# Reciprocal softmax sums spread over head rows by a DRAM round trip in place of 0/1 matmuls

## The chip, the cores and the metric

The kernel runs on one core of a Trainium2 chip. The metric is the device time of one execution in microseconds (us), the median of three runs; smaller is better. Engines are named as in the profile: PE (TensorE, matrix products; PEld its weight loads), DVE (VectorE), ACT (ScalarE), POOL (GpSimd), SP (SyncE, which here only issues DMAs).

## The reference

A two-layer encoder trunk for 1024 tokens of width 1024 in float32. Layer 0 mixes tokens by grouped-query softmax attention (16 query heads, 4 key/value heads of width 64), layer 1 by a chunked gMLP; each is followed by a squared-ReLU MLP, and each sub-layer is normalised, modulated and gated by a conditioning vector. What matters here:

```python
s = jnp.einsum('bqkgd,bskd->bkgqs', q_blk, k).astype(jnp.float32) * scale
p = jax.nn.softmax(s, axis=-1).astype(v.dtype)
o = jnp.einsum('bkgqs,bskd->bqkgd', p, v)
...
return o @ w_o          # added to x, times a gate
```

The softmax is written as exponentials, their product with v, and a division of every row of o by the row's sum of exponentials. The change is in how that division reaches the transposed o.

## The kernel before, in words

x is held transposed, features on partitions and tokens along the row, in two halves of 512 tokens. A float32 product is made of three fast products: each operand is split into a high part (ACT cast to fp32r) and a low part (the rest, by DVE or POOL), and hi·hi, hi·lo and lo·hi are added up in PSUM.

**Attention.** 64 units, each one head and 256 queries; the first 32 units are half 0. A unit has scores (L948) and their maximum (L951, DVE), exponentials (L957, ACT, which also leaves the row sums in `rowsum`), transposes (L965), their split (L968 ACT, L974 DVE), the product with v (L984) and copies of the output (L994, L996 ACT, L1001 POOL) into `ot`: per pair of heads `dt` and half one buffer of 128 rows (64 per head) x 512 queries, not yet divided. The stages of three neighbouring units are interleaved by the string `ORDER` (line 1784); most of them are pinned to their place on their engine. Its last item, `m00`, is where other work is slipped in, one piece a unit. The output projection's preparation for half 0 stands there from unit `WO_AT` = 53 on: at unit 53 `copy_sel`, at unit 54 `wo_sums(0)`, at units 55 to 62 `wo_prep(0, dt)` for dt = 0 to 7. Units 64 and 65 of the loop are the tail of the last two.

**The division before.** `wo_sums` takes the reciprocal of the row sums (queries on partitions, heads along the row), splits it into high and low part (L882, L883), transposes it by four PE transposes into 32 rows (16 heads, high and low) x 512 queries (L886) and copies that out of PSUM (L888, ACT). `sel` is a constant 32 x 1024 matrix of 0 and 1, loaded from DRAM (two DMAs) and cast by ACT (L875). `wo_prep(hf, dt)` multiplies 128 columns of it with the transposed reciprocals on PE (L892, the tile `bc`): every row of the 128 gets its head's reciprocals. DVE multiplies `ot` by `bc` (L894), and the result is split (L896 ACT; L897, POOL in half 0, DVE in half 1).

**The projection.** `wo_mm(m, halves)`: 24 products per half of 128x512 (L906 to L908: eight k, three products each), then DVE adds the gated result to x (L910, the evacuation), and the square of the new x is summed (L260 ACT, L264 DVE). m = 0 to 5 run for half 0 alone, m = 6 and 7 for both halves, then m = 0 to 5 for half 1. m = 0 is emitted at the attention's end. `wo_sums(1)` comes next, and `wo_prep(1, dt)` three, three and two at a time ahead of m = 1, 2, 3 (`PREP`). `mods` slips in loads and products (L145, L153, L158, L166) that make the modulation vectors of later layers.

**Weights.** `load_w` keeps one weight ahead (`AHEAD` = 1): `issue_w` has SP load a 128x1024 float32 buffer `w` (L113), ACT cast its high part (L116) and POOL take the low part (L117) into two `s` buffers. There are four `w` buffers, which the modulation's loads share, and five `s`, of which one holds the conditioning vector. SP issues in program order, and a DMA waits at the head of its queue until its buffer is free; a buffer `w` of a weight comes free with its L117, one of the modulation with its L153. A DMA also waits for the eighth DMA before it on its queue.

Of the kernel before, what the change touches and what calls it, by code (L numbers as in the profile page):

```python
# [28 lines left out]

INS = (  # L30
    "xT", "cond", "cols", "ada", "adan", "wqkv", "qkg", "wo", "wu", "wv", "bv", "ws", "bs", "wgo", "wi",
    "wm", "rope", "sel",
)


# [1 line left out]
def encoder_kernel(ctx: ExitStack, tc: tile.TileContext, t: dict, out: bass.AP):  # L37
# [3 lines left out]
    const = ctx.enter_context(tc.tile_pool(name="const", bufs=1))  # L41
    small = ctx.enter_context(tc.tile_pool(name="small", bufs=3))
    mem = ctx.enter_context(tc.tile_pool(name="mem", bufs=1))

    uid = [0]

# [4 lines left out]
    def pin(ins):  # L51
        tc.keep_in_program_order(ins)
# [7 lines left out]
    def slot(dt=F32, shape=(P, 512)):  # L60
        return mem.tile(list(shape), dt, tag="t", name=nm("t"), bufs=SLOTS["t"])
# [24 lines left out]
    def f32(ap):  # L86
        return ap.bitcast(F32)
# [771 lines left out]


    on = {}
    sel = []
    ot = {}
    rT = {}

    def load_sel():
        for i in range(2):
            raw = slot(F32, (32, 512))
            nc.sync.dma_start(raw, t["sel"][:, i * 512 : (i + 1) * 512])
            sel.append(raw)  # L870

    def copy_sel():
        for i in range(2):
            s_ = slot(F32R, (32, 512))
            pin(S.copy(s_, sel[i]))  # L875
            sel[i] = s_

    def wo_sums(hf):
        ri = small.tile([P, 4, NH], F32, tag="ri", name=nm("ri"), bufs=1)
        V.reciprocal(ri, rowsum[:, 4 * hf : 4 * hf + 4])  # L880
        rs = small.tile([P, 4, 2, NH], F32R, tag="rs", name=nm("rs"), bufs=1)
        V.tensor_copy(rs[:, :, 0], ri)  # L882
        V.tensor_tensor(rs[:, :, 1], ri, f32(rs[:, :, 0]), ALU.subtract)  # L883
        pt = bank_x("rt", (32, 512), F32R)
        for j in range(4):
            T.transpose(pt[:, j * P : (j + 1) * P], rs[:, j].rearrange("p s h -> p (s h)"), identr)  # L886
        rT[hf] = slot(F32R, (32, 512))
        S.copy(rT[hf], f32(pt))  # L888

    def wo_prep(hf, dt):  # L890
        pb = bank_x("bc")
        T.matmul(pb, sel[dt // 4][:, (dt % 4) * P : (dt % 4 + 1) * P], rT[hf], start=True, stop=True)  # L892
        o_ = ot.pop((dt, hf))
        V.tensor_tensor(o_, o_, pb, ALU.mult)  # L894
        hi, lo = slot(F32R), slot(F32R)
        S.copy(hi, o_)  # L896
        (G, V)[hf].tensor_tensor(lo, o_, f32(hi), ALU.subtract)  # L897
        on[(dt, hf)] = (hi, lo)
# [17 lines left out]
    with ExitStack() as es:  # L916
# [132 lines left out]
        for i in range(nu + 2):  # L1049
# [7 lines left out]
            for op in ORDER.split():  # L1057
                f, w, j = op[0], int(op[1]), int(op[2])
                if f == "m":
                    if i in deferred:  # L1060
                        deferred.pop(i)()
                    elif i == WO_AT - 6:
                        load_sel()
                    elif WO_AT <= i < WO_AT + 10:
                        if i == WO_AT:
                            copy_sel()
                        elif i == WO_AT + 1:
                            wo_sums(0)
                        else:
                            wo_prep(0, i - WO_AT - 2)  # L1070
                    elif i >= nu:
                        mods(1)
                    if late_mods and i % 4 == 1:
                        late_mods.pop()()
                    if i % 4 == 3 and 12 <= i < 52:
                        late_mods.append(mod_ahead())
                    slabs.step(bank_x, i >= 14 and (i % 4 in (1, 2) or i % 8 == 3))
                elif f == "q":
                    if i % 4 == 0 and w == 0 and i + 4 < nu:
                        qh = q_stage(units[i + 4].qq, units[i + 4].g)  # L1080
                    if i % 4 > 1 and w == 1 and i + 2 < nu:
                        q_trans(qh, i % 4 - 2, nxt)
                else:
                    u = (u0, u1, u2)[w]
                    if u and (i or f not in "se"):
                        stages[f](u, j)
# [6 lines left out]

    es_a.close()
    p_y = ctx.enter_context(tc.tile_pool(name="p_y", bufs=4, space=PSUM))
    dram = ctx.enter_context(tc.tile_pool(name="dram", bufs=1, space=bass.MemoryType.DRAM))

    class Out:


# [305 lines left out]
        out_.run(at_out, done)  # L1406

    wo_sums(1)
    for m in range(1, WA):
        if m == 1:  # L1410
            x[1] = [load_x(1, k) for k in range(KT)]
        for dt in PREP[m - 1] if m < 4 else ():
            wo_prep(1, dt)
        wo_mm(m, (0,), bank_y)
        mods(WOM[m])
# [371 lines left out]
def _pack(inp):  # L1787
# [35 lines left out]
    cos, sin = np.cos(ang), np.sin(ang)  # L1823
    rope = np.stack([np.concatenate([cos, cos], -1), np.concatenate([-sin, sin], -1)]).astype(np.float32)
    t["rope"] = rope.reshape(2, 8, P, HD).transpose(0, 2, 1, 3).reshape(2, P, 512)
    sel = np.zeros((32, KT, P), np.float32)
    for dt in range(KT):
        for m in range(P):
            sel[2 * dt + m // 64, dt, m] = 1.0
            sel[16 + 2 * dt + m // 64, dt, m] = 1.0  # L1830
    t["sel"] = sel.reshape(32, KT * P)
    return {k: np.ascontiguousarray(t[k]) for k in INS}


# [16 lines left out]
```

## Time and profile before

| | |
|---|---|
| time of three runs | 2626.04, 2627.94 (median), 2629.11 us |
| span of the profiled execution, first to last instruction | 2625.8 us |
| busy: PE, PEld, DVE, ACT, POOL | 2601.6, 2172.2, 2183.1, 1451.1, 723.2 us |
| mean granted TensorE clock | 0.999 of full speed |
| attention's units with work of the projection's preparation | about 470 to 555 us |
| projection, half 0 and m = 6, 7 | about 548 to 608 us |

The profiled execution's own time isn't stated beside its page; its span lies 0.2 to 3.3 us below the three times, which is what an execution has around its first and last instruction, and the scatter. How to read the rows: in a timeline, start, length, engine, line, operation, out<-in with the buffer numbers left out, and in brackets how long the engine was idle before and what released it. In the rows of groups, the total busy time and the mean ns of one, then the engine's idle time just before them. In the rows of windows, the window, its length, and for each engine its busy time and number of instructions, then the granted clock, the share of the DMA engines in use and GB/s. Lines are those of the kernel before.

### The profile page before, as it was taken

Reading aid. Unit: us, or ns where it says so; the run is one execution under the profiler, and the core shown is the slowest. Engines: PE = TensorE matmul, PEld = TensorE weight load, DVE = VectorE, ACT = ScalarE, POOL = GpSimd, SP = SyncE. Lnnn points to the kernel's source line nnn. Section 1 sums busy time; section 2 is a strip of 40 time slices with the busy share of each in tenths; the row PEclk is TensorE's granted clock in tenths of the full one; section 3 lists DMA queues with packets and bytes.
Section 4 is the critical chain, followed back from the end, with each engine's and each line's share of the span. In section 5 each row is a group of like instructions: output and inputs, shape, how many; then the busy total and the mean of one; then the engine's idle time right before and its main releaser. Section 6 shows DMA issues by size and latency. Waiting matters only on the chain. (4 is left out here: it accounts for less than half of the span.)

```text
span 2625.8 us, 37307 instructions
## 1 busy us (share of the span) xinstructions
PE 2601.6 (99%) x12860; PEld 2172.2 (83%) x12860; DVE 2183.1 (83%) x3276; ACT 1451.1 (55%) x2612; POOL 723.2 (28%) x531
## 2 busy tenths in 40 slices
PE   9999999999999999999999999999999999999999
PEld 7789999888788888888888888888888788888887
DVE  7868999887989989877897687788979977789974
ACT  4569999854654455446543354445456645465442
POOL 0238776533000004430122054451520000005400
PEclk9999999999999999999999999999999999999999
DMA  8010222234486788545243355568641554487461
GB/s 306 27 33 9 74 88 75 97 112 145 168 288 245 270 310 306 192 133 172 82 136 121 120 174 175 178 204 305 237 141 50 177 179 156 153 310 268 149 211 58
DMA packets 208752, 435.39 MB, mean 166 GB/s; under 512 B 23025, under 2 KB 35441, under 8 KB 208562
## 3 DMA queue, kind: packets, MB, share of 16 engines
q1 hardware_dynamic: 181682, 395.24, 44.7%
q10 hardware_dynamic: 26880, 37.76, 4.0%
q8 instruction: 102, 1.67, 0.3%
q14 instruction: 88, 0.72, 0.1%
HBM read 310.23 MB, written 122.68 MB: 165 GB/s over the span
## 5 line engine op out<-in xcount | busy, mean ns | idle before, releaser
L1212 PE MATMUL out<-t,s 128*128 128x512 f32 x1232 | 479.9, 390 | 0.9 <-ACT t L328 0.8
L1213 PE MATMUL out<-t,s 128*128 128x512 f32 x1232 | 479.3, 389 | 0.7 <-DVE t L329 0.7
L1214 PE MATMUL out<-t,s 128*128 128x512 f32 x1232 | 478.9, 389 | 0.0
L469 PE MATMUL w<-t,s 128*128 128x512 f32 x1168 | 459.8, 395 | 0.9 <-ACT t L328 0.5
L470 PE MATMUL w<-t,s 128*128 128x512 f32 x1168 | 455.2, 390 | 1.8 <-DVE t L329 1.8
L471 PE MATMUL w<-t,s 128*128 128x512 f32 x1168 | 454.7, 389 | 0.0
L329 DVE TENSOR_TENSOR t<-t,t 128x512 fp32r<-128x512 f32 x408 | 324.7, 806 | 36.2 <-ACT t L328 29.0
L328 ACT CAST t<-t 128x512 fp32r<-128x512 f32 x408 | 245.3, 617 | 122.2 <-DMA t<-hf 71.7
L1213 PEld LDWEIGHTS out<-t,s 128*128 128x128 f32 x1232 | 231.2, 188 | 50.2 <-DVE t L329 1.8
L1212 PEld LDWEIGHTS out<-t,s 128*128 128x128 f32 x1232 | 231.2, 188 | 50.2 <-ACT t L328 1.7
L1214 PEld LDWEIGHTS out<-t,s 128*128 128x128 f32 x1232 | 231.2, 188 | 48.1
L454 ACT CAST s<-w 128x512 fp32r<-128x512 f32 x292 | 173.4, 616 | 161.4 <-PE w L471 104.3
L470 PEld LDWEIGHTS w<-t,s 128*128 128x128 f32 x1168 | 219.3, 188 | 49.7 <-DVE t L329 5.2
L469 PEld LDWEIGHTS w<-t,s 128*128 128x128 f32 x1168 | 219.3, 188 | 49.4 <-issue 2.9
L471 PEld LDWEIGHTS w<-t,s 128*128 128x128 f32 x1168 | 219.2, 188 | 45.6
L455 DVE TENSOR_TENSOR s<-w,s 128x512 fp32r<-128x512 f32 x292 | 221.8, 766 | 41.1 <-ACT s L454 40.6
L1194 ACT CAST s<-t 128x512 fp32r<-128x512 f32 x240 | 148.2, 620 | 187.0 <-PE out L1214 136.3
L1180 POOL TENSOR_TENSOR w<-w,t 128x512 f32<-128x512 f32 x20 | 34.2, 1721 | 767.7 <-DMA t<-hf 691.5
L1195 DVE TENSOR_TENSOR s<-t,s 128x512 fp32r<-128x512 f32 x240 | 195.1, 814 | 56.1 <-ACT s L1194 55.4
L951 DVE TENSOR_REDUCE mx<-s 128x1 f32<-128x1024 f32 x128 | 156.2, 1220 | 30.5 <-PE s L948 29.2
L974 DVE TENSOR_TENSOR t<-t,t 128x512 fp32r<-128x512 f32 x256 | 164.1, 681 | 17.1 <-ACT t L968 16.4
L984 PE MATMUL o<-t,t 128*128 128x256 f32 x1024 | 162.6, 291 | 0.0
(251 smaller groups left out, 5089.1 us busy)
## 6 DMA issues: line engine op xcount, KB each, us to landing
t<-hf SPq DMA_DIRECT2D x320, 256.0 KB, 4.0
hf<-c SPq DMA_DIRECT2D x156, 256.0 KB, 3.4
w<-in_wi_dram SPq DMA_DIRECT2D x64, 512.0 KB, 4.5
hf<-c ACTq DMA_DIRECT2D x96, 256.0 KB, 2.7
w<-in_ada_dram SPq DMA_DIRECT2D x36, 512.0 KB, 3.9
x<-in_ada_dram SPq DMA_DIRECT2D x64, 256.0 KB, 5.4
t<-in_wm_dram SPq DMA_DIRECT2D x64, 256.0 KB, 4.7
wf<-w SPq DMA_DIRECT2D x64, 256.0 KB, 3.0
```

Source lines behind the costliest of these rows:

```text
L328: S.copy(hi, src)
L329: (eng or V).tensor_tensor(lo, src, f32(hi), ALU.subtract)
L454: S.copy(hi, src)
L455: V.tensor_tensor(lo, src, f32(hi), ALU.subtract)
L469: T.matmul(ps, hi[:, a], th, start=kt == 0, stop=False)
L470: T.matmul(ps, hi[:, a], tl, start=False, stop=False)
L471: T.matmul(ps, lo[:, a], th, start=False, stop=kt == 3)
L974: pin(V.tensor_tensor(lo, pt, f32(hi), ALU.subtract))
L1195: V.tensor_tensor(lo, src, f32(hi), ALU.subtract)
L1212: T.matmul(ps, hi[:, a], th, start=begin and kt == 0, stop=False, **g)
L1213: T.matmul(ps, hi[:, a], tl, start=False, stop=False, **g)
L1214: T.matmul(ps, lo[:, a], th, start=False, stop=end and kt == 3, **g)
```

## The change

The reciprocals are transposed as plain float32, 16 rows x 512 queries, copied out by ACT, and stored to a DRAM tile `rd`. For each pair of heads two DMAs read one row of it each, 64 times over, into the two halves of a 128x512 buffer; DVE multiplies `ot` by that buffer, in SBUF. `sel`, its loads and casts, the split of the reciprocals and the sixteen `bc` products are gone. In half 0 `wo_sums(0)` is at unit 53, the loads for dt = 0 to 7 at units 54 to 61, each one unit ahead of its `wo_prep`, which stay at units 55 to 62. In half 1 all eight pairs of loads are issued behind `wo_sums(1)`, ahead of the loop over m.

```diff
     def wo_sums(hf):
         ri = small.tile([P, 4, NH], F32, tag="ri", name=nm("ri"), bufs=1)
         V.reciprocal(ri, rowsum[:, 4 * hf : 4 * hf + 4])
-        rs = small.tile([P, 4, 2, NH], F32R, tag="rs", name=nm("rs"), bufs=1)
-        V.tensor_copy(rs[:, :, 0], ri)
-        V.tensor_tensor(rs[:, :, 1], ri, f32(rs[:, :, 0]), ALU.subtract)
-        pt = bank_x("rt", (32, 512), F32R)
+        pt = bank_x("rt", (NH, 512))
         for j in range(4):
-            T.transpose(pt[:, j * P : (j + 1) * P], rs[:, j].rearrange("p s h -> p (s h)"), identr)
-        rT[hf] = slot(F32R, (32, 512))
-        S.copy(rT[hf], f32(pt))
+            T.transpose(pt[:, j * P : (j + 1) * P], ri[:, j], ident)
+        rT = slot(F32, (NH, 512))
+        S.copy(rT, pt)
+        rd[hf] = dram.tile([NH, 512], F32, name=nm("rd"))
+        nc.sync.dma_start(rd[hf], rT)
+
+    def wo_load(hf, dt):
+        rb_[(dt, hf)] = slot()
+        for i in range(2):
+            nc.sync.dma_start(rb_[(dt, hf)][64 * i : 64 * i + 64],
+                              rd[hf][2 * dt + i : 2 * dt + i + 1].broadcast_to([64, 512]))
 
     def wo_prep(hf, dt):
-        pb = bank_x("bc")
-        T.matmul(pb, sel[dt // 4][:, (dt % 4) * P : (dt % 4 + 1) * P], rT[hf], start=True, stop=True)
         o_ = ot.pop((dt, hf))
-        V.tensor_tensor(o_, o_, pb, ALU.mult)
+        V.tensor_tensor(o_, o_, rb_.pop((dt, hf)), ALU.mult)
...
-                    elif i == WO_AT - 6:
-                        load_sel()
-                    elif WO_AT <= i < WO_AT + 10:
-                        if i == WO_AT:
-                            copy_sel()
-                        elif i == WO_AT + 1:
-                            wo_sums(0)
-                        else:
+                    elif i == WO_AT:
+                        wo_sums(0)
+                    elif WO_AT < i < WO_AT + 10:
+                        if i < WO_AT + 9:
+                            wo_load(0, i - WO_AT - 1)
+                        if i > WO_AT + 1:
                             wo_prep(0, i - WO_AT - 2)
...
     wo_sums(1)
+    for dt in range(KT):
+        wo_load(1, dt)
     for m in range(1, WA):
```

Lines behind the change shift: the weight's load is L114 in the new kernel (L113 before), its cast L117, its low part L118, the modulation's load L146 and product L154, the squares L265; the store is L875, the broadcast loads L880, the multiplication L885, the split L887 and L888, the evacuation L901, the unit's copies L985 and L987, the exponential L948.

Where the order on an engine moves, at three places. First SP's queue at the attention's end, in the kernel before; `w<-in_wo` are the projection's weights (w_7224 is m = 3, w_7278 m = 4, w_7318 m = 5, w_7361 m = 6), `w<-in_ada` the modulation's:

```order
113 L145 DMA w_7198<-in_ada_dram 128x1024
114 L113 DMA w_7224<-in_wo_dram 128x1024
115 L145 DMA w_7259<-in_ada_dram 128x1024
116 L113 DMA w_7278<-in_wo_dram 128x1024
117 L145 DMA w_7313<-in_ada_dram 128x1024
118 L113 DMA w_7318<-in_wo_dram 128x1024
119 L145 DMA w_7353<-in_ada_dram 128x1024
120 L145 DMA w_7357<-in_ada_dram 128x1024
121 L113 DMA w_7361<-in_wo_dram 128x1024
```

The same place of SP's queue in the changed kernel (w_7234 is m = 3, w_7284 m = 4, w_7324 m = 5):

```order
120 L146 DMA w_7214<-in_ada_dram 128x1024
121 L114 DMA w_7234<-in_wo_dram 128x1024
122 L875 DMA rd_7117<-t_7115 16x512
123 L146 DMA w_7269<-in_ada_dram 128x1024
124 L880 DMA t_7119<-rd_7117 64x512 x2
...
131 L880 DMA t_7140<-rd_7117 64x512 x2
132 L114 DMA w_7284<-in_wo_dram 128x1024
133 L146 DMA w_7319<-in_ada_dram 128x1024
134 L114 DMA w_7324<-in_wo_dram 128x1024
```

The store and the sixteen loads of half 1 stand between the weights of m = 3 and m = 4; the modulation's load that goes ahead of m = 5 (w_7319) takes the buffer of an earlier one, w_7209, and waits for its product on DVE.

Second, DVE at the evacuations of half 0, in the kernel before (x_6945 is m = 1, x_6947 m = 2; w_7193 and w_7198 are products of the modulation):

```order
653 L910 SCALAR_TENSOR_TENSOR x_6945<-wo_7164,mod,x_6945 128x512
654 L894 TENSOR_TENSOR t_4968<-t_4968,bc_7203 128x512
655 L894 TENSOR_TENSOR t_5148<-t_5148,bc_7210 128x512
656 L264 TENSOR_TENSOR t_7059<-t_7059,t_7190 128x512
657 L153 SCALAR_TENSOR_TENSOR w_7193,mod<-w_7193,s_110 128x1024
...
662 L153 SCALAR_TENSOR_TENSOR w_7198,mod<-w_7198,s_110 128x1024
663 L894 TENSOR_TENSOR t_5316<-t_5316,bc_7217 128x512
664 L158 TENSOR_TENSOR mod<-mod,cols 128x1
665 L910 SCALAR_TENSOR_TENSOR x_6947<-wo_7230,mod,x_6947 128x512
```

And DVE in the changed kernel (x_6948 is m = 2, x_6950 m = 3; t_7119 to t_7140 are the broadcast buffers):

```order
647 L901 SCALAR_TENSOR_TENSOR x_6948<-wo_7240,mod,x_6948 128x512
648 L885 TENSOR_TENSOR t_4970<-t_4970,t_7128 128x512
649 L885 TENSOR_TENSOR t_5150<-t_5150,t_7131 128x512
650 L885 TENSOR_TENSOR t_5318<-t_5318,t_7134 128x512
...
654 L888 TENSOR_TENSOR t_7171<-t_4806,t_7170 128x512
655 L901 SCALAR_TENSOR_TENSOR x_6950<-wo_7290,mod,x_6950 128x512
656 L265 TENSOR_TENSOR t_7060<-t_7060,t_7206 128x512
657 L154 SCALAR_TENSOR_TENSOR w_7209,mod<-w_7209,s_112 128x1024
```

The product that frees the buffer for the load ahead of m = 5 stood ahead of the evacuation of m = 2; it now stands behind that of m = 3.

Third, ACT at the cast of the first projection weight, in the kernel before (s_7023<-w_7021):

```order
634 L968 CAST t_6318<-t_6313 128x512
635 L116 CAST s_7023<-w_7021 128x1024
636 L968 CAST t_6331<-t_6326 128x512
637 L957 ACTIVATE c_6333,rowsum<-s_6304,mx_6309 128x1024
638 L994 COPY t_4968<-o_6281 64x256
639 L996 COPY t_6346<-o_6281 64x256
```

In the changed kernel (s_7024<-w_7022):

```order
634 L948 ACTIVATE c_6330,rowsum<-s_6301,mx_6306 128x1024
635 L985 COPY t_4970<-o_6278 64x256
636 L987 COPY t_6343<-o_6278 64x256
637 L117 CAST s_7024<-w_7022 128x1024
638 L887 CAST t_6356<-t_1905 128x512
```

The cast stood ahead of a unit's second exponential; it now stands behind it and behind the unit's copies.

More of the change, by code (lines that the diff above doesn't have):

```diff
@@ L31 @@
     "xT", "cond", "cols", "ada", "adan", "wqkv", "qkg", "wo", "wu", "wv", "bv", "ws", "bs", "wgo", "wi",
-    "wm", "rope", "sel",
+    "wm", "rope",
 )
@@ L43, in encoder_kernel @@
     mem = ctx.enter_context(tc.tile_pool(name="mem", bufs=1))
+    dram = ctx.enter_context(tc.tile_pool(name="dram", bufs=1, space=bass.MemoryType.DRAM))
     uid = [0]
@@ L861, in encoder_kernel @@
     on = {}
-    sel = []
+    rd, rb_ = {}, {}
     ot = {}
[L864 to L876, printed above, removed]
     def wo_sums(hf):
@@ L1095, in encoder_kernel @@
     p_y = ctx.enter_context(tc.tile_pool(name="p_y", bufs=4, space=PSUM))
-    dram = ctx.enter_context(tc.tile_pool(name="dram", bufs=1, space=bass.MemoryType.DRAM))
     class Out:
@@ L1825, in _pack @@
     t["rope"] = rope.reshape(2, 8, P, HD).transpose(0, 2, 1, 3).reshape(2, P, 512)
[L1826 to L1831, printed above, removed]
     return {k: np.ascontiguousarray(t[k]) for k in INS}
```

## The prediction

> **What bounds the kernel now.** I read the page first, then the windows of the attention's second half and of the output projection, then the timelines of PE, ACT, POOL and the DMA queue there. From the page:
>
> ```profile
> span 2625.8 us, 37307 instructions
> PE 2601.6 (99%) x12860; PEld 2172.2 (83%) x12860; DVE 2183.1 (83%) x3276; ACT 1451.1 (55%) x2612; POOL 723.2 (28%) x531
> ```
>
> PE is idle for 24.2 us of the whole program, so time is saved only by taking work from PE or by closing one of its few gaps, and any new gap adds to the time almost one for one. The change touches 470 to 600 us. Two windows of one unit each (one head, 256 queries), the first ahead of the output projection's preparation, the second within it; the columns are length, then busy time and count of PE, PEld, DVE, ACT and POOL, the granted clock, the DMA share and GB/s:
>
> ```profile
> 448.50:454.00 5.50, 5.50 (x43) 5.11 (x42) 5.15 (x7) 5.09 (x11) 0.72 (x1) 1.00 0.00 1
> 526.30:532.40 6.10, 6.10 (x43) 5.32 (x42) 5.51 (x8) 5.59 (x12) 1.97 (x2) 1.00 0.01 3
> ```
>
> A plain unit takes 5.50 us and a unit with a broadcast matmul 6.10; PE is full in both. In the second, ACT has 5.59 and DVE 5.51 us of work. If PE's share falls, ACT is next, at about 5.6 to 5.7.
>
> **The change part by part.** The groups in 470 to 600 us that it touches or that wait behind it (busy time, mean ns, idle before):
>
> ```profile
> L892 PE MATMUL bc<-t,t 32*128 32x512 f32 x16 | 6.6, 459 | 0.2 <-ACT t L888 0.2
> L894 DVE TENSOR_TENSOR t<-t,bc 128x512 f32<-128x512 f32 x16 | 10.6, 678 | 0.3 <-PE bc L892 0.3
> L116 ACT CAST s<-w 128x1024 fp32r<-128x1024 f32 x8 | 8.4, 1049 | 17.1 <-DMA w<-in_wo_dram 10.8 <-PE wo L907 6.3
> L117 POOL TENSOR_TENSOR s<-w,s 128x1024 fp32r<-128x1024 f32 x8 | 20.8, 2601 | 35.1 <-ACT s L116 30.3 <-PE bc L892 4.8
> L153 DVE SCALAR_TENSOR_TENSOR w<-w,s 128x1024 f32<-128x1024 f32 x12 | 14.6, 1215 | 0.0
> ```
>
> What a broadcast matmul costs PE is the distance of the starts around it, not its 459 ns. PE's timeline, one of half 0, then the three groups of half 1, the first and the last with the matmuls around them:
>
> ```profile
> 490.37 0.49 PE L892 MATMUL bc<-t,t 32*128 32x512 f32 x1
> 490.79 1.20 PE L948 MATMUL s<-x,t 128*128 128x512 f32 x4
> ...
> 556.42 0.40 PE L907 MATMUL wo<-t,s 128*128 128x512 f32 x1
> 557.02 0.95 PE L892 MATMUL bc<-t,t 32*128 32x512 f32 x3 [0.20 <-ACT t L888]
> 557.90 0.50 PE L908 MATMUL wo<-t,s 128*128 128x512 f32 x1
> ...
> 562.43 0.96 PE L892 MATMUL bc<-t,t 32*128 32x512 f32 x3
> ...
> 568.45 0.39 PE L907 MATMUL wo<-t,s 128*128 128x512 f32 x1
> 568.68 0.39 PE L908 MATMUL wo<-t,s 128*128 128x512 f32 x1
> 569.00 0.73 PE L892 MATMUL bc<-t,t 32*128 32x512 f32 x2
> 569.65 0.50 PE L906 MATMUL wo<-t,s 128*128 128x512 f32 x1
> ```
>
> *Half 0, eight matmuls gone from eight units.* From its start to that of the next matmul it is 490.79 - 490.37 = 0.42 us, and 8 x 0.42 = 3.4. The floor that ACT sets (5.6 to 5.7 against 6.10) lets nearly all of it through, 0.4 to 0.5 a unit. I take 3.4.
>
> *Half 1, eight matmuls gone in groups of 3, 3 and 2.* The usual pitch is 568.68 - 568.45 = 0.23. The first group holds PE for 557.90 - 556.42 - 0.23 = 1.25 (a wait for the copy of the transposes among it), the last for 569.65 - 568.68 - 0.23 = 0.74, which is 0.37 a matmul; the middle group by that 1.1. Sum 3.1 us.
>
> *An awkward unit.* ACT's timeline, with the copies that end two units one behind the other:
>
> ```profile
> 491.69 0.37 ACT L996 COPY t<-o 64x256 f32<-64x256 f32 x1
> 497.85 1.05 ACT L116 CAST s<-w 128x1024 fp32r<-128x1024 f32 x1 [2.27 <-DMA w<-in_wo_dram]
> 500.90 0.37 ACT L996 COPY t<-o 64x256 f32<-64x256 f32 x1
> ```
>
> The unit that ends at 500.90 is 9.21 us long: ACT's cast of the first projection weight stands ahead of an exponential and waits 2.27 us for its load. What PE and the granted clock do then:
>
> ```profile
> 500.55 1.59 PE L965 MATMUL t<-ident,c 128*128 128x128 f32 x7 [1.89 <-ACT c L957]
> 501.79 2.06 PE L948 MATMUL s<-x,t 128*128 128x512 f32 x4
> ...
> 500.00:502.00 2.00, 1.45 (x8) 1.46 (x9) 1.24 (x2) 1.96 (x6) 2.00 (x4) 0.69 0.00 0
> 502.00:504.00 2.00, 2.00 (x7) 1.51 (x7) 0.75 (x2) 2.00 (x4) 2.00 (x4) 0.50 0.69 168
> ```
>
> PE stalls for 1.89 us and then runs at a clock of 0.50: four matmuls take 2.06 where they took 1.20 at 490.79. After the change this cast stands behind the unit's exponential and its copies. Of the 9.21 - 6.10 = 3.1 us, the cast itself (1.05) stays in ACT's time; I let the other 2.1 go, and keep 0 as the other end, since a late weight can then hold the next unit's casts instead. The Trainium skill (TensorE: Matmul & The Clock Gate, "What's actually happening") has the clock fall after an idle window of about 3.4 us; here it fell after 1.89 us, so the measurement decides, and short stalls are to be feared as well.
>
> *The loads of half 0.* The store and sixteen loads go on SP's queue, which waits there mostly for others' buffers. A load is asked for one unit, 5.5 us, ahead of its multiplication. The nearest rows for landing, and for issuing (four loads in one row):
>
> ```profile
> hf<-t SPq DMA_DIRECT2D x44, 256.0 KB, 2.2
> x<-in_cond_dram SPq DMA_DIRECT2D x2, 256.0 KB, 5.8
> w<-in_wo_dram SPq DMA_DIRECT2D x14, 512.0 KB, 3.7
> 487.47 1.75 SPq L520 DMA_DIRECT2D x<-in_xT_dram  x4
> ```
>
> A store takes 2.2 us to land, a broadcast load (in_cond is one) up to 5.8, an issue 1.75 / 4 = 0.44. So a load is at most 0.3 us late per unit; I cost it at nothing, with the unit's 5.5 us as cover. If that cover fails, the multiplication waits on DVE with the next unit's maxima (L951) behind it, and through them the exponentials: 8 x 0.3 = 2.4 us as the upper end. The store waits on SP for ACT's copy of the transposes; behind it stand loads of x and of the modulation, which have units of time.
>
> *The multiplication and the small things.* It takes 678 ns reading PSUM; with both operands in SBUF the squares of L264 are the nearest row:
>
> ```profile
> 564.40 2.05 DVE L264 TENSOR_TENSOR t<-t,t 128x512 f32<-128x512 f32 x1
> 574.68 0.68 DVE L264 TENSOR_TENSOR t<-t,t 128x512 f32<-128x512 f32 x1
> 563.49 2.42 POOL L117 TENSOR_TENSOR s<-w,s 128x1024 fp32r<-128x1024 f32 x1 [4.83 <-PE bc L892]
> 576.45 2.91 POOL L117 TENSOR_TENSOR s<-w,s 128x1024 fp32r<-128x1024 f32 x1 [3.63 <-ACT s L116]
> ```
>
> The same instruction takes 0.68 us alone and 2.05 while POOL's subtraction runs (563.49 to 565.91), ending with it. So a multiplication lasts 0.68 to about 2.4 us; at half 0 the window of 526.30 has only 1.97 us of POOL's work in two pieces, and DVE has 0.2 to 0.6 us a unit over; at half 1 nothing on PE waits directly for it. I take zero, and 2 us as the other end. The transposes, the copy and the selector's two casts change by some tenths, off or on either side: zero.
>
> *Half 1: sixteen loads ahead of a weight.* This is the cost. SP's issues of the projection weights m = 3, 4, 5, 6 in the kernel before:
>
> ```profile
> 557.87 0.33 SPq L113 DMA_DIRECT2D w<-in_wo_dram  x1
> 565.93 0.33 SPq L113 DMA_DIRECT2D w<-in_wo_dram  x1
> 570.12 0.33 SPq L113 DMA_DIRECT2D w<-in_wo_dram  x1
> 579.39 0.33 SPq L113 DMA_DIRECT2D w<-in_wo_dram  x1
> ```
>
> From issue to use a weight needs its landing (3.7), ACT's cast (1.05) and POOL's subtraction (2.4 to 2.9): about 7.2 us, and 9.2 for m = 5 (570.12 to 576.45 + 2.91 = 579.36). PE uses one up in 24 x 0.23 = 5.5 us. So the weights are just in time in the kernel before: m = 5 is ready at 579.36 and PE starts it at about 569.65 + 2 x 5.5 = 580.6.
>
> Reckon from the end of m = 1 on PE, called 0 (562.43 before, where the second group starts). The load of m = 3 goes out 562.43 - 557.87 = 4.6 us ahead of it, and 3.3 ahead once the first group's 1.25 is gone. Behind it stand the store, landed by -3.3 + 0.4 + 2.2 = -0.7, and the sixteen loads at 0.33 to 0.44 each, 5.3 to 7 us, taken 6.7: to 6.0. Then comes the load of m = 4, which before went out 565.93 - 562.43 = 3.5 us after that point, when POOL had done m = 3. It is ready at 6.0 + 7.2 = 13.2, and PE asks for it at 2 x 5.5 + 0.2 = 11.2, the 0.2 being the first product, which needs no low part: **stall 2.0** (m = 3 ends at 11.0, m = 4 at 18.5).
> The load of m = 5 now stands behind a modulation load whose buffer comes free by a product (L153 above, 1.2 us) that DVE has behind the evacuation of m = 3 and the squares after it (0.7 each): 11.0 + 0.7 + 0.7 + 1.2 = 13.6, and the two issues make 14.4. As POOL is then through with m = 4 (13.2), nothing else holds it. With the 9.2 us of m = 5 it is ready at 23.6, with 7.2 at 21.6; PE asks for it at 18.7. I take 23, since the product will queue behind the multiplications: **stall 4.3**. The load of m = 6 waits for the buffer of m = 5 and goes out at 23, is ready at 30.2, asked for at 23 + 5.5 = 28.5: **stall 1.7**. From there on a weight serves two halves, 11 us, and PE is not late again. Sum 8.0 us. Bounds: 3, if the loads cost SP little and the product comes early; 11, if they run at the rate of eight in flight, 5.8 / 8 = 0.73 each, 5 us more than 6.7, of which the chain passes some 3 on.
>
> **Sum:** -3.4 - 3.1 - 2.1 + 8.0 = -0.6 us. The span would be 2625.2. The three runs shown (2626.04 to 2629.11) lie 0.2 to 3.3 above that span, their median 2.1; the forecast is 2627.94 - 0.6 = 2627.3, no change that can be measured: 0.2% or 5.3 us is about what a measurement of this kernel tells from none. With its bounds (gain 6.5 to 8.6, cost 3 to 11) the case runs from 2622.3 to 2632.4.
>
> **The rivals.**
> *The weights are not late* (faster). SP's own waits:
>
> ```profile
> SPq L113 <- POOL s L117: 21.9, 5, 7.6
> ```
>
> If SP issues the loads while it would have waited for POOL anyway (five waits, 7.6 us the longest), and the product that frees the modulation's buffer runs early, nothing is put on PE, and the whole gain of 8.6 us stays: 2619.3. For it: the longest wait exceeds the 6.7 us of issues. Against it: they can begin only after the store has landed, and the order on DVE is fixed.
> *The clock falls behind each stall* (slower). The row at 502 shows PE at 0.50 after 1.89 us without work. The three stalls at their upper end of 11 us, each followed by some 2 us at half clock, that is 1.7 us lost with the ramp (2.06 - 1.20 = 0.86 for four matmuls, twice), would cost 11 + 3 x 1.7 = 16.1 against a gain of 8.6: +7.5 us, 2635.4. It decides from stalls that cost over 8.6 + 5.3 = 13.9 us with their slow clock. Against it: slow matmuls of m = 5 give the weight of m = 6 time to arrive, so that the losses overlap. By the Trainium skill's window (same page and section) of 3.4 us only the stall of 4.3 us would bring it, and it would cost 1.7 us, not 5.1.
> *No easing of the awkward unit.* Then 2.1 us less are gained, 2629.4, still no measurable change; it is within the main case.
>
> **How the numbers follow.** Main case (stalls eat the gain): 0.60. Weights in time: 0.22. Slow clock behind the stalls: 0.18. All of the main case's range is within 5.3 us of 2627.94, so faster 0.22, same 0.60, slower 0.18. The range reaches from 2619 (the first rival's value) to 2634, which leaves out the far part of the second rival.
>
> **What would show it.** In the profile after: no bc group, units of 5.6 to 5.8 us from 491 to 545, the stall before 500 gone or moved to ACT's later casts; on SP the sixteen loads in one run of about 6.7 us between the loads of m = 3 and m = 4; PE waiting for POOL's L118 at the starts of m = 4, 5 and 6 by some 2, 4 and 2 us, and the granted clock below 1 behind the second. I am wrong if PE shows no such waits (then the change gains over 5.3 us), or if DVE stands waiting for the broadcast loads and holds the evacuations or the attention's maxima behind it.

## The result, and the profile after

The changed kernel takes 2633.49 us, the median of seven runs (2629.82 to 2637.97), against 2627.94 for seven runs of the kernel before, measured beside it. That is 5.6 us more by the medians, and 7.4 by the ratio of 1.0028 (95% interval 1.0018 to 1.0037; 0.0028 x 2628), where no measurable change was forecast. The profiled execution is one of the slower of the seven (2637.46 us); its span is 2635.7 us, 9.9 above that of before:

```profile
span 2635.7 us, 37348 instructions
PE 2600.6 (99%) x12844; PEld 2173.8 (82%) x12844; DVE 2185.2 (83%) x3272; ACT 1450.8 (55%) x2610; POOL 725.1 (28%) x531
```

PE is busy 1 us less and idle 11 us more: the products are gone, and waits have come. Where? Three landmarks are in all kernels of this study: the copy that ends an attention unit near 443 us, the copy that ends the last unit, and SP's first load of the next MLP's weights (in_wi). Before, then after:

```profile
443.02 0.37 ACT L996 COPY t<-o 64x256 f32<-64x256 f32 x1
556.00 0.37 ACT L996 COPY t<-o 64x256 f32<-64x256 f32 x1
616.35 18.99 SPq L416 DMA_DIRECT2D w<-in_wi_dram  x4
```

```profile
444.55 0.37 ACT L987 COPY t<-o 64x256 f32<-64x256 f32 x1
555.17 0.37 ACT L987 COPY t<-o 64x256 f32<-64x256 f32 x1
624.20 13.54 SPq L417 DMA_DIRECT2D w<-in_wi_dram  x3
```

From the first to the second (the attention with half 0's preparation) it was 112.98 us and is 110.62: 2.4 less. From the second to the third (the projection with half 1's) it was 60.35 and is 69.03: 8.7 more. So 6.3 us come from the places of the change. The other 3.6 lie before the first landmark (1.5) and behind the third (2.1), where the change has no work of its own; they are not put down to it.

PE's waits of over 1 us in these two stretches, from the timeline (idle time and releaser in brackets). Before, there was one, of 1.89 us.

```profile
465.96 0.66 PE L956 MATMUL t<-ident,c 128*128 128x128 f32 x4 [1.07 <-DVE t L965]
505.99 1.11 PE L956 MATMUL t<-ident,c 128*128 128x128 f32 x4 [3.93 <-DVE t L965]
576.49 0.79 PE L897 MATMUL wo<-t,s 128*128 128x512 f32 x1 [5.18 <-ACT s L117]
578.99 0.79 PE L899 MATMUL wo<-t,s 128*128 128x512 f32 x1 [1.27 <-POOL s L118]
594.73 0.50 PE L899 MATMUL wo<-t,s 128*128 128x512 f32 x1 [2.27 <-POOL s L118]
```

The third and fourth are for the weight of m = 4 (high part, low part), the fifth for that of m = 6: the chain of weights, as feared, and 8.7 us in sum. SP's queue, and two windows of six us (the granted clock is the third column from the right), say why it is so long:

```profile
557.05 0.33 SPq L114 DMA_DIRECT2D w<-in_wo_dram  x1
557.47 0.38 SPq L875 DMA_DIRECT2D rd<-t  x1
...
560.62 10.05 SPq L880 DMA_DIRECT2D t<-rd  x16
570.77 0.54 SPq L114 DMA_DIRECT2D w<-in_wo_dram  x1
...
578.96 0.33 SPq L114 DMA_DIRECT2D w<-in_wo_dram  x1
```

```profile
576.00:582.00 6.00, 4.23 (x9) 2.94 (x10) 6.00 (x12) 2.52 (x5) 2.42 (x1) 0.50 0.55 181
582.00:588.00 6.00, 6.00 (x24) 4.77 (x24) 5.97 (x10) 2.10 (x3) 2.78 (x1) 0.84 0.65 205
```

The sixteen loads take SP 10.05 us, so the weight of m = 4 goes out at 570.77, when PE is at the last products of m = 3. The clock falls within the long wait and is 0.50 over the whole first window (in windows of 0.4 us: from about 573.6 to 583.9): PE does 9 products in it, with 1.27 us of waiting, and 24 in the next, where its full pace of 0.23 us gives 26.

### The profile page after: what moved, and what is told of

It reads as the page before. It is cut to its first block, busy times and chain, and to the rows that moved or that the text cites. A ratio compares the mean times of both kernels' runs of the same rounds, so it can differ in the third digit from the quotient of the medians.

```text
span 2635.7 us, 37348 instructions
## 1 busy us (share of the span) xinstructions
PE 2600.6 (99%) x12844; PEld 2173.8 (82%) x12844; DVE 2185.2 (83%) x3272; ACT 1450.8 (55%) x2610; POOL 725.1 (28%) x531
## 3 DMA queue, kind: packets, MB, share of 16 engines
q8 instruction: 101, 1.65, 0.3%
```

## The experiments

Theory A, after the traces: the loss is made in half 1, where SP issues sixteen broadcast loads ahead of a weight. The rivals: B, the attention's stall makes it; C, the order on DVE makes it, with multiplications that wait for loads ahead of evacuations and of the products that free buffers; A1 against A2, whether a load's price is its issue or its bytes. Ratios are to the kernel before, measured beside each, with 95% intervals; "attention" and "projection" are the two stretches between the landmarks against those of before (112.98 and 60.35), each from one profile.

| kernel | ratio | attention | projection |
|---|---|---|---|
| changed kernel | 1.0028 [1.0018, 1.0037] | -2.4 | +8.7 |
| e1, half 0 alone | 0.9992 [0.9984, 1.0001] | -3.9 | +0.3 |
| e2, half 1 alone | 1.0032 [1.0020, 1.0043] | -1.2 | +10.4 |
| e3, loads spread | 1.0050 [1.0037, 1.0062] | -5.1 | +16.0 |
| e4, eight loads in half 1 | 1.0010 [1.0001, 1.0019] | -3.9 | +6.0 |
| e5, loads behind m = 6 | 1.0022 [1.0013, 1.0031] | -3.0 | +7.3 |
| e6, half 0 at unit 44 | 1.0017 [1.0008, 1.0026] | | +0.2 |
| e7, before, with unused loads | 1.0022 [1.0013, 1.0031] | -1.3 | +7.1 |
| e8, before, with tiny unused loads | 1.0028 [1.0017, 1.0038] | -1.7 | +7.5 |
| e9, half 0 at unit 48 | 1.0013 [1.0004, 1.0022] | | +0.2 |
| e10, half 0 at unit 50 | 0.9997 [0.9988, 1.0006] | | +0.5 |
| e11, one load a half | 1.0035 [1.0021, 1.0049] | -1.8 | +8.0 |
| e12, no round trip, SBUF operand | 0.9994 [0.9985, 1.0003] | -4.3 | +1.6 |
| e13, no round trip, PSUM operand | 0.9992 [0.9983, 1.0001] | -3.7 | -0.2 |

The attention of e2, e7 and e8 does the same work as before and still shows -1.2 to -1.7: that much of this column is scatter.

**e1 and e2: one half at a time.** In e1 the functions of before serve half 1, in e2 half 0:

```diff
-    wo_sums(1)
-    for dt in range(KT):
-        wo_load(1, dt)
+    wo_sums_b(1)          # e1: half 1 by the products of before
```

> Half 0 by the DRAM round trip, half 1 by the 0/1 products as before. Theory A (the loss is made in half 1, where SP issues sixteen broadcast loads ahead of a projection weight): half 0 alone gains, as in the two traces, 3.6 us over the units from 477 to 545 less 1.3 for a product that met POOL at 463, so about 2 to 3.5 us below the kernel before, 2624.5 to 2626, and no wait of PE for weights m = 4 to 6. Rival B (the loss is the attention's 3.9 us stall at 502 to 506 and its slow clock): not faster than before, 2628 to 2633.

> Half 0 by the 0/1 products as before, half 1 by the DRAM round trip. Theory A: the whole loss is here, 8.7 us between the points 545 and 615 of the two traces: 2636.6, PE waiting over 5 us at the start of m = 4 and over 2 us at m = 6. Rival B: half 1 gains its 3.1 us of products, 2624.8.

2624.26 us in e1 (the kernel before beside it: 2626.87) and 2635.24 in e2, both close to theory A. Rival B falls: with half 0 alone the attention's stall is there (2.44 us at 503.24) and the kernel is no slower. Half 1 alone carries the whole loss.

**e4: half as many loads, the same bytes.** In half 1:

```diff
+        if hf:
+            nc.sync.dma_start(rb_[(dt, hf)], rd[hf][2 * dt : 2 * dt + 1].broadcast_to([P, 512]))
+            return
```

> The changed kernel with half 1's loads as eight of 128 rows in place of sixteen of 64: both heads of a pair get the first head's reciprocals, so the bytes are the same and the issues half. Theory A1 (the number of issues on SP is the price, 0.59 us each): the run of loads takes 4 to 5 us instead of 10, the weight of m = 4 is issued 5 to 6 us sooner, and the stall at m = 4 falls from 5.5 to about 1 us. The product behind the evacuation of m = 3 still delays m = 5, by up to 4.5: together 2628 to 2630, some 4 us below the changed kernel. Rival A2 (the bytes are the price: the loads go out as earlier ones land): the run still takes about 10 us and the time stays at 2633.

2629.56 us. SP and ACT's cast of m = 4 in e4:

```profile
557.52 4.02 SPq L880 DMA_DIRECT2D t<-rd  x8
562.32 0.33 SPq L114 DMA_DIRECT2D w<-in_wo_dram  x1
```

```profile
568.88 1.04 ACT L117 CAST s<-w 128x1024 fp32r<-128x1024 f32 x1 [2.79 <-DMA w<-in_wo_dram]
```

The run of loads falls from 10.05 to 4.02 us and the weight goes out in time, as A1 has it; 2.7 us of the projection's 8.7 come back. But PE still waits for m = 4, 1.64 us for its high part and 2.73 for its low part, where about 1 us was expected: the weight needs 6.6 us to land (562.32 to 568.88) behind loads of 256 KB, where it was 3.4 in the kernel before (565.93 to 569.29). The time is as expected, the wait is not; behind long loads their bytes have a price too.

**e7 and e8: the loads by themselves.** The kernel before, with the store and sixteen loads into buffers that nobody reads, of 512 numbers a row (e7) or 16 (e8):

```diff
     wo_sums(1)
+    rd = dram.tile([NH, 512], F32, name=nm("rd"))
+    nc.sync.dma_start(rd, f32(rT[1])[:NH])
+    for dt in range(KT):
+        rb = slot()
+        for i in range(2):
+            nc.sync.dma_start(rb[64 * i : 64 * i + 64, :512],
+                              rd[2 * dt + i : 2 * dt + i + 1, :512].broadcast_to([64, 512]))
```

> The kernel before with its 0/1 products, and beside them the store and the sixteen broadcast loads of half 1 at the same place of SP's queue, into buffers that nobody reads: work is added, none taken away, and DVE's order stays that of before. Theory A (the loads themselves hold up the weight of m = 4, on SP and on the way through DMA): its load goes out at about 570.7 in place of 565.9 and PE waits 3 to 4 us at the start of m = 4, with a slow clock behind it: 3.5 to 5.5 us above the kernel before. Rival C (it is the multiplications waiting in DVE's order): nothing waits for these loads, at most 0.5 us above.

> As the kernel before with unused loads, but each of the sixteen loads reads 16 numbers of a row in place of 512: 4 KB each in place of 128 KB. A1 (the price is the issue on SP, about 0.59 us whatever the size): the run of loads takes 9 us again and the loss is that of the full loads, 3.5 to 5.5 us. A2 (the price is the bytes): the run takes 5 to 6 us, the weight of m = 4 lands in its usual 3.4 us, and the loss is at most 1 us.

2632.64 and 2634.06 us, against 2626.14. The loads' own rows, e7, then e8 (duration of the issue in ns, least, median, most):

```profile
L1413 SPq DMA_DIRECT2D t<-rd x16: 444/584/602, 559.0 to 568.7; - x16
DMA to landing us min/median/max: 2.7/3.0/4.0
```

```profile
L1413 SPq DMA_DIRECT2D t<-rd x16: 444/584/596, 559.3 to 569.0; - x16
DMA to landing us min/median/max: 2.2/2.3/2.6
```

An issue takes 0.584 us whether it moves 128 KB or 4 KB. The loss is alike, 6.5 and 7.9 us by the medians, and more than the 3.5 to 5.5 that was expected. PE's products are untouched and nobody reads the loads, so these alone are enough for a loss of that size, by their issue on SP: in e7 the weight of m = 4 goes out at 569.43, 0.1 us behind the last of them, and PE waits 2.00 and 1.63 us for it. A1 holds. C is not shut out by these two, since DVE's instructions are those of before but their order is not. The modulation's product that ran at 566.38 before, ahead of the evacuation of m = 2 (572.75), stands behind that evacuation in e7:

```profile
566.71 0.75 DVE L911 SCALAR_TENSOR_TENSOR x<-wo,mod,x 128x512 f32<-128x512 f32 x1 [4.03 <-PE wo L909]
...
570.98 1.22 DVE L154 SCALAR_TENSOR_TENSOR w<-w,s 128x1024 f32<-128x1024 f32 x1
```

PE does not wait for the weight of m = 5 there, so this order is not seen to cost anything in e7.

**e11: the change without the loads.** One pair of loads a half serves all pairs of heads:

```diff
     def wo_load(hf, dt):
+        if dt:
+            rb_[(dt, hf)] = rb_[(0, hf)]
+            return
```

> The changed kernel with one pair of broadcast loads a half in place of eight: all pairs of heads are divided by the sums of the first pair, so fourteen loads of each half are left out and all else of the change stays. Theory A (the loads' issues are the whole cost, the products without them a gain): half 1 gains its 3.1 us and half 0 at least the 3.7 us that it gained with its loads: 6 to 9 us below the kernel before, 2618 to 2621, and PE waits nowhere between m = 1 and m = 6. Rival C (multiplying from SBUF, where POOL can hold DVE up, and DVE's order cost it): no more than 3 us below.

2634.62 us (before: 2626.52): theory A falls as the only cause. DVE, then POOL, then SP in e11:

```profile
561.46 0.75 DVE L904 SCALAR_TENSOR_TENSOR x<-wo,mod,x 128x512 f32<-128x512 f32 x1 [3.24 <-PE wo L902]
564.89 1.90 DVE L888 TENSOR_TENSOR t<-t,t 128x512 f32<-128x512 f32 x3 [2.68 <-DMA t<-rd]
...
570.91 1.22 DVE L154 SCALAR_TENSOR_TENSOR w<-w,s 128x1024 f32<-128x1024 f32 x1
572.06 2.84 DVE L891 TENSOR_TENSOR t<-t,t 128x512 fp32r<-128x512 f32 x1
```

```profile
569.70 4.65 POOL L118 TENSOR_TENSOR s<-w,s 128x1024 fp32r<-128x1024 f32 x1 [4.82 <-ACT s L117]
```

```profile
564.91 0.34 SPq L114 DMA_DIRECT2D w<-in_wo_dram  x1
574.38 0.33 SPq L146 DMA_DIRECT2D w<-in_ada_dram  x1
574.80 0.38 SPq L114 DMA_DIRECT2D w<-in_wo_dram  x1
```

Now the weight of m = 4 goes out in time (564.91). But the first multiplication starts at 564.89, behind the evacuation of m = 1, where before three multiplications were done ahead of that evacuation (557.97 to 559.85 in its trace). DVE has stood idle for 3.24 and 2.68 us by then. Twelve of its sixteen multiplications and splits follow in one heap without a pause, up to 577.4; the modulation's product comes at 570.91 inside it, POOL's low part of m = 4 takes 4.65 us beside DVE's instructions from SBUF, and the load of m = 5 goes out at 574.80. PE waits 1.65 us for m = 4, 1.09 and 1.70 for m = 5, and 2.74 for m = 6. Two theories were left: L, the latency of store and load makes the heap; P, the operand in SBUF makes it.

**e12 and e13: no round trip in half 1.** One product sums all heads' reciprocals into 128 rows, from SBUF (e12, with ACT's copy) or straight from PSUM (e13); the loop of loads is gone (not printed):

```diff
+        if hf:
+            pb = bank_x("bc")
+            T.matmul(pb, ones[:NH], rT, start=True, stop=True)
+            one = pb              # e12: one = slot(); S.copy(one, pb)
+            for dt in range(KT):
+                rb_[(dt, hf)] = one
+            return
```

> Half 0 by the DRAM round trip. In half 1 there is no store and no load: one product of PE adds up all heads' reciprocals into 128 rows, ACT copies it to SBUF, and all eight multiplications read that copy (the division is by a wrong sum; the work of DVE, ACT and POOL is that of the changed kernel). Theory L (the round trip's latency: DVE stands idle for it after the evacuation of m = 1 and then has its multiplications and splits in one heap, behind which the modulation's products and with them the buffers come late): the heap is gone, half 1 gains 2 to 3 us, 4 to 7 us below the kernel before. Theory P (multiplying from SBUF, where DVE and POOL hold each other up, so that POOL's low parts of the weights take 3 to 5 us in place of 2.4): still as slow as the kernel with one load, 5 to 9 us above the kernel before.

> The same without ACT's copy: the eight multiplications read the product in PSUM; the order on DVE is the same instruction for instruction. By both theories 4 to 7 us below the kernel before. What differs between the two runs is the price of the operand in SBUF: nothing by theory L (but for 0.6 us of ACT), 9 us or more by theory P.

2625.14 and 2623.36 us, against 2626.93: the loss is gone in both. The order on DVE is the same in the two, but it is not that of e11: five multiplications stand ahead of the evacuation of m = 1, where e11 has none. So the runs show the cost of the round trip together with the later place that the multiplications have on DVE with it; they do not part the two. (The store and one pair of loads, 1.5 us on SP, are also gone from half 1; the weight of m = 4 was in time in e11.) In this sense L holds, and P fails as the main cause: the operand, with ACT's copy, costs 1.8 us of the projection's stretch in the profiles, and nothing that the runs resolve. But the gain of 4 to 7 us is missing as well. The window 560 to 580 of e12, then of e13, and e13's one long wait (the low part of m = 6):

```profile
560.00:580.00 20.00, 18.97 (x84) 15.20 (x83) 19.87 (x31) 6.58 (x10) 7.46 (x3) 1.00 0.48 160
```

```profile
560.00:580.00 20.00, 20.00 (x90) 16.45 (x89) 18.56 (x29) 7.26 (x11) 7.38 (x4) 1.00 0.52 163
```

```profile
581.69 0.50 PE L906 MATMUL wo<-t,s 128*128 128x512 f32 x1 [1.19 <-POOL s L118]
```

e13 lacks the second and third groups of products (1.1 + 0.74 us by the prediction's rows) and gets 1.19 of it back as a wait for a weight. Counted from the copy that ends the last unit, it starts m = 5 1.8 us sooner than the kernel before (22.84 us against 24.65) and the second half of m = 6 only 0.3 us sooner (35.26 against 35.53). So half 1 gains next to nothing: the chain of weights through SP, ACT and POOL is hardly faster than PE with its products. In e12 PE waits 1.03 and 1.55 us for low parts, and DVE is busy for 19.87 of 20 us.

**e3 and e5: the loads elsewhere.** e3 puts three, three and two pairs of loads behind m = 1, 2, 3, e5 all behind the issue of m = 6's weight; the loop of loads ahead is gone, and the multiplications move behind their loads (not printed):

```diff
         wo_mm(m, (0,), bank_y)
+        for dt in PREP[m - 1] if m < 4 else ():     # e3; e5: if m == WA - 1, all eight
+            wo_load(1, dt)
```

> The changed kernel, with half 1's loads three, three and two at a time behind the projection of m = 1, 2, 3 and its multiplications one m later, so that six, six and four loads stand between weights in place of sixteen. Theory A: the weights come in time again but for tenths, and the 3.1 us of products stay gained: 2621 to 2624. Rival C (the order on DVE costs it: multiplications that wait for loads hold the evacuations and the modulation's products, whose buffers the weights need): the waits move to m = 2 to 5 and cost as much, 2630 to 2634.

> The changed kernel with half 1's sixteen loads behind the weight of m = 6 on SP and its multiplications ahead of m = 6, so that no load stands ahead of a weight that is needed within 5 us. Theory A: the weights m = 3 to 6 come in time; what may be late instead is the second half of m = 6, whose multiplications stand on DVE behind the evacuation of its first half: a wait of 3 to 5 us there, and 1 to 4 us below the kernel before. Rival C (it is DVE's order of multiplications, evacuations and modulation, wherever the loads stand): the stall is as long as in the changed kernel, 4 to 7 us above the kernel before.

2639.56 and 2632.2 us. In e3 six loads stand ahead of the weight of m = 3, which had been free of them, and PE waits for it:

```profile
554.51 3.65 SPq L880 DMA_DIRECT2D t<-rd  x6
...
559.36 0.38 SPq L114 DMA_DIRECT2D w<-in_wo_dram  x1
```

```profile
567.71 0.79 PE L897 MATMUL wo<-t,s 128*128 128x512 f32 x1 [5.20 <-ACT s L117]
```

The weight needs 7.3 us from its issue to the start of its cast at 566.61, again in the company of loads, six ahead of it and six behind. Of e5, theory A's wait in the second half of m = 6 is there (3.12 us), but the whole is 7.3, more than it gave; three other waits, of 1.2 to 1.5 us, stand beside it. Both expectations of A were too good. e5 is 6.1 us above the kernel before, which is what rival C gave (4 to 7), with no load ahead of the weights m = 3 to 6; two of its waits (1.20 and 3.12 us) are for results of the multiplications. e3, 12.7 us above, is slower than either theory gave.

**e6, e9, e10: half 0 earlier.** `WO_AT` = 44, 48 and 50 in e1's kernel, with `sel` loaded later:

```diff
-WO_AT = 53
+WO_AT = 44
```

> As the kernel with only half 0 changed, and half 0's preparation nine units earlier (the sums at unit 44, the multiplications at units 46 to 53), so that its loads are over before the loads of x and of the first projection weights begin. If the attention's stall at about 501 to 503 (2.4 us with half 0 changed, 1.9 before) comes from the broadcast loads that compete with the first weight, it shrinks to under 1 us: 1.5 to 3 us below that kernel, about 4 to 6 us below the kernel before. Rival: the weight and the loads of x alone make it, as in the kernel before: the same time as with half 0 changed in place, 2 to 3 us below the kernel before.

> Only half 0 changed, its preparation five units earlier than in the changed kernel (sums at unit 48, multiplications at units 50 to 57): behind the attention units in which POOL makes the modulation's products, and with half of its loads over before the first projection weight is loaded. If those two are what half 0's loads and products collide with, both the stall of 1.1 us at 463 and that of 2.4 us at 501 shrink: 4 to 7 us below the kernel before. Rival: every unit that takes a multiplication and its split is at its floor already and the stalls only move: 1 to 3 us below, as with half 0 changed in place.

> The same with the sums at unit 50. By the first theory between the two, 3 to 6 us below the kernel before; by the rival 1 to 3 us below.

2631.14 us (before 2626.14) for e6; 2631.43 and 2626.62 (before 2627.56) for e9 and e10. From the copy that ends a unit at 406.85 to the last one it is 149.15 us before, 0.9 more in e6, 3.1 more in e9 and 3.1 less in e10. None beats e1, and the earlier ones are slower: e6 and e9 came 5.0 and 3.9 us above the kernel before, where theory and rival both had them below it. (In e9 the clock is at 0.50 from 485.8 to 496.1, behind a stall of 2.56 us.) The stretch 440 to 490 in e6, then in e1:

```profile
440.00:490.00 50.00, 43.59 (x312) 38.91 (x312) 47.94 (x62) 43.74 (x88) 42.62 (x31) 1.00 0.26 78
```

```profile
440.00:490.00 50.00, 48.69 (x365) 44.89 (x363) 44.50 (x59) 44.42 (x90) 29.65 (x24) 1.00 0.17 57
```

In e6 the stall beside the first weight is gone, but DVE and POOL (47.94 and 42.62 of 50) hold up PE among POOL's products of the modulation. The stalls move, as the rival said, though at a price that it did not have. The best that came of all this, e1, is at 0.9992, which the runs can't tell from the kernel before.

## Why the prediction was wrong

The mechanism was named, sixteen loads ahead of a weight, but the sum missed by 6.9 us: -0.6 forecast, +6.3 measured in the two stretches. The gain was taken at 8.6 and is 5.5 (2.4 in the attention, 3.1 of products in half 1); the cost was taken at 8.0 and is 11.8 (the 8.7 of projection above, and the 3.1 of products on top). Two steps failed. The sum put the slow clock at nothing, although its own row showed it behind a stall of 1.89 us: it costs 3.1 us. And it let 2.1 us of the awkward unit go, which came to 0.3, while a wait that it has no term for took 1.3 in another unit. The stalls themselves, 8.0, came to 8.7, but that they agree is luck: 2.0, 4.3 and 1.7 were reckoned for m = 4, 5 and 6, and it was 6.45, 0 and 2.27, the first of them for an issue of the loads that was taken too short. The range of the main case, up to 2632.4, also left out the 2.4 and 2 us that the working had kept as the upper ends for late loads and for the multiplication. Term by term:

- **Half 0's products, -3.4: right.** From 507.61 to 544.84 before, six units took 37.23 us, 6.21 each; after, 509.30 to 544.01, 5.79 each. That is 0.42 a unit, as worked out. PE is still full, with ACT and DVE right below: from 527.50 to 532.91 they are busy for 5.41, 5.37 and 5.32 of 5.41 us.
- **The awkward unit, -2.1: wrong.** The cast did move behind the exponential, and the unit became 5.69 us long; the next one became 9.92 (6.71 before). Together they took 15.92 us and take 15.61. ACT's rows in the changed kernel:

```profile
499.38 0.37 ACT L987 COPY t<-o 64x256 f32<-64x256 f32 x1
501.82 1.04 ACT L117 CAST s<-w 128x1024 fp32r<-128x1024 f32 x1 [2.07 <-DMA w<-in_wo_dram]
...
503.68 1.05 ACT L117 CAST s<-w 128x1024 fp32r<-128x1024 f32 x1 [0.29 <-DMA w<-in_wo_dram]
...
509.30 0.37 ACT L987 COPY t<-o 64x256 f32<-64x256 f32 x1
```

  The wait for the weight is 2.07 us, where it was 2.27; it now holds the casts of the next unit's transposes, and PE's stall grew from 1.89 to 3.93. The prediction had kept 0 as the other end for this very reason, and should have taken it: a wait moved along a queue is a wait still. Single profiles scatter here: the two units take 14.15 us in e1, with the order of after, and 14.85 in e2, with that of before.
- **A product of the modulation, +1.3: not in the sum.** It ran at 476.43 before, in 1.22 us. In the changed kernel it stands earlier on DVE and lasts 2.55 us beside POOL's work; PE waits 1.07 us for the split behind it, and the unit takes 6.80 us in place of 5.55:

```profile
462.75 2.55 DVE L226 SCALAR_TENSOR_TENSOR w<-w,s 128x1024 f32<-128x1024 f32 x1
```

  Every kernel here whose half 0 is changed at this place has this wait (1.07 to 1.11 us); why the product moved, no run shows.
- **The loads of half 0, at nothing: nearly right.** They land after 5.2 us in the median and 10.0 at most, where 5.8 was taken as the most, and one multiplication waits 1.60 us for its load. It is hardly what the attention lost: in e11, with one pair of loads, PE still waits 1.70, 1.49 and 1.66 us between 499 and 508.
- **Half 1's products, -3.1: right on PE, and worth little there.** PE starts m = 3 at 565.71, 10.54 us behind the copy that ends the last unit, where it was 13.65 (569.65): 3.1 less.

```profile
565.71 0.39 PE L897 MATMUL wo<-t,s 128*128 128x512 f32 x1
```

  e13 shows that such time comes back as a wait for weights that are just in time.
- **Sixteen loads: the issue was mis-sized.** Taken at 0.42 us, between the issues of a weight (0.33) and of x (0.44), it is 0.584 (e7, e8), and the run takes 10.05 us in place of 6.7. That lies within the bound of 0.73 by landing, but landing isn't the reason: loads of 4 KB land sooner and take as long to issue. The stall at m = 4 was put at 2.0; it is 5.18 + 1.27.
- **m = 5 behind DVE's product, 4.3: not seen here, real without the loads.** The load of m = 5 goes out at 578.96, when POOL is through with m = 4 (576.52 + 2.42). That is 18.5 us behind the evacuation of m = 1 (560.47), where 14.4 behind its end was reckoned; but m = 4 is late and slow itself, and PE does not wait for m = 5. In e11, without the run of loads, it does, 1.09 and 1.70 us.
- **m = 6, 1.7: it is 2.27.**
- **The slow clock, at nothing in the sum: 3.1.** It was kept for a rival, with 1.7 us for each of three stalls. It came in the attention too, behind the wait of 3.93, and in the projection once, for longer than was thought. Fifteen distances between products, from 576.49 to this row, take 7.84 us, 6.57 without the wait of 1.27, where 15 x 0.23 = 3.45 is the usual:

```profile
584.33 0.40 PE L897 MATMUL wo<-t,s 128*128 128x512 f32 x1
```

  The waits of 8.7 and these 3.1 make up the 11.8.
- **The multiplication from SBUF**, taken at nothing: 1.8 us of the projection (e12 against e13, ACT's copy included), within the 2 us kept as its end.

The loss has two causes that don't add: sixteen issues ahead of a weight (shown by e7 and e8), and the round trip, behind which DVE's work comes late and in a heap (shown by e11 against e12). Either alone costs 6 to 8 us of the projection: 7.1 and 7.5 in e7 and e8 against the kernel before, 6.4 in e11 against e12 (8.0 - 1.6). Left open is how much of e11's loss is the latency, how much the order on DVE that came with it, and how much POOL's longer low parts within the heap; no kernel parted these.

## What to carry to other kernels

Where a stream of weights is just in time, a step that is freed on the busiest engine gains nothing until the stream is faster, and whatever is put ahead of a weight on its queue is paid as soon as it makes the weight late. Count DMAs by issues on the queue before counting bytes, with a row of the same shape if there is one. Where the clock falls behind a stall of PE, slow products come on top of the wait, and they belong into the sum. A value that comes by way of DRAM comes microseconds later than one from a matrix product: look at what its consumer does meanwhile, and what is then done in one heap.

## What the runs showed of the hardware

- The issue of a broadcast load into 64 rows holds SP's queue for 0.584 us at 128 KB and at 4 KB (e7, e8), one into 128 rows for 0.383 (median in e4, 4.02 us for the eight of them), a plain load of a weight for 0.33.
- A store of 32 KB and a load of it back: in e11 the store is issued at 558.45 and the first multiplication starts at 564.89, 6.4 us later, and 8.35 us behind the start of the copy of the transposes (556.54). Before, that copy and a product gave DVE its operand within 1.6 us of the copy's start (556.39 to 557.97).
- The granted clock fell to 0.50 behind stalls of 1.89 us (before), 2.31 us (e13, at 502.13), 3.93 and 5.18 us (after), and stayed at 1.00 behind 2.24 us in e12 (at 503.16) and 2.44 us in e1, whose window reads:

```profile
500.00:510.00 10.00, 7.40 (x55) 6.39 (x54) 7.43 (x11) 9.79 (x18) 7.97 (x5) 1.00 0.49 157
```

  So the length of a stall alone doesn't decide. The Trainium skill (TensorE: Matmul & The Clock Gate, "What's actually happening") has an activity window of about 3.4 us and calls it free-running, by which the phase would matter too. The time at 0.50 agrees with such a window: it lasts 3.4 us before (500.8 to 504.2) and 10.2 us, three times as long, in the changed kernel (573.6 to 583.9). That the fall comes after at least one idle window, as the Trainium skill has it there, doesn't agree: 1.89 us without work were enough in the kernel before. What decides, no run here shows.
- POOL's subtraction of 2.4 us took 4.65 beside DVE's instructions with both operands in SBUF (e11). The Trainium skill (SBUF — State Buffer, "Who interferes with whom") has a DVE instruction with two SBUF inputs contend with a GpSimd instruction that reads SBUF, and calls the shared port pair an exclusive lock. The rows agree with the two taking turns: DVE goes on at its usual pace from 569.71 to 572.06, 2.35 us, and then its split, usually 0.69 us, takes 2.84 and ends 0.55 us behind POOL (574.90 against 574.35).
